# Column sums of the five transitions: from running sums on VectorE and GpSimd to one set of matmuls per tile

## The chip, the core and the metric

The kernel runs on one core of a Trainium2 chip. The core has a matrix engine (TensorE, "PE" in the rows; its weight loads are listed apart as "PEld"), VectorE ("DVE"), ScalarE ("ACT"), GpSimd ("POOL") and SyncE ("SP", which issues DMAs). The metric is the device time of one execution in microseconds (us); lower is better. All times here come from the hardware profiler on the chip or from timed runs.

## The reference, cut to what matters

A network of three layers on 256 tokens of 1024 features in fp32. Each of its residual steps ends with a sum over the 1024 features of each token: the layer norms need the sum and the sum of squares, the second block's norm after the mixer needs sums of squares.

```python
def layer_norm(x, g, b):
    xf = x.astype(jnp.float32)
    mu = jnp.mean(xf, axis=-1, keepdims=True)
    var = jnp.mean(jnp.square(xf - mu), axis=-1, keepdims=True)
    return ((xf - mu) * lax.rsqrt(var + EPS) * g + b).astype(x.dtype)
...
        x = layer_norm(ALPHA * x + (1.0 + g1[:, None, :]) * y, ln_g[l, 0], ln_b[l, 0])
        h = modulate(x, sh2, sc2)
        y = sq_relu_mlp(h, mlp_w1[l], mlp_w2[l])
        x = layer_norm(ALPHA * x + (1.0 + g2[:, None, :]) * y, ln_g[l, 1], ln_b[l, 1])
...
    mix = jnp.concatenate([o_dn, o_at.astype(o_dn.dtype)], axis=-1) @ w_out[l]
    h = h + rms_norm_2(mix, norm_mix_post[l])
    u = rms_norm_2(h, norm_mlp_pre[l])
```

## The kernel before, in words

Activations lie feature-major: 1024 features are eight tiles (m = 0 to 7) of 128 partitions by 256 tokens. Every big product keeps fp32 accuracy by three matmuls: `mm3` (L387 to L389) multiplies high part by high part, and each high part by the other's low part. ScalarE casts a weight's high part (`cast_hi`, L347) and VectorE, or in one place GpSimd, takes the low part (`cast_lo`, L352). In the rows `hi` and `lo` are a weight's parts, `oh`/`ol` and `acth`/`actl` the activation's, and `y` a product tile in PSUM, two tiles to a bank.

**Transitions.** Where one product ends and a norm must be known before the next begins, `tail` (L702) runs. There are five, called T1 to T5 here: T1 after `ev_out` (around 204 to 220 us), T2 after layer 0's MLP (396 to 414), T3 after `od_out` (527 to 551), T4 after layer 1's MLP (727 to 752), T5 after `b_out` (943 to 970). T1 to T4 are layer norms, closed by `ln_finish` or a sibling that uses it; T5 is `post_norm`. A transition holds back the last three weights (two in T3), multiplies all but the last of them into four tiles first, and then takes the tiles in the order 0, 2, 4, 6, 1, 3, 5, 7, each finished by the last weight: three matmuls for the first four tiles, nine for the later ones (six in T3); the scheduler may move the others ahead. When tile m is complete, VectorE forms the residual tile (`zn` in the rows, L633; `full` in T5, L1870) and ScalarE its square (`sq`, L635 and L1871; T5 also has `sqn`, L1872).

**Sums.** `totals` adds tiles up on an engine: the n-th tile of the group 0 to 3 onto the first (L556, L559), again for 4 to 6, and the eighth stays alone. Residuals are added on VectorE and squares on GpSimd; in T5 `full` on GpSimd, `sq` and `sqn` on VectorE. The running sums are the tiles `run`. Only at n = 7 does TensorE sum over features: `col_sum` (L543, recorded at L392) makes a 128x128 fp32 piece of the tile the stationary operand and multiplies it by a column of ones, two matmuls a tile (256 tokens), added up in the PSUM tile `tr`. Such a matmul has two records in the profile. `warm` (L392 with `zero`, PSUM tile `pj`) issues matmuls of zeros. Then VectorE reads `tr` (L585, T5 L1885) and the statistics follow.

**The other edits' places.** `tail` casts the first two weights of the next stage ahead: the low part of the second is GpSimd's. `rest1` (T3 and what follows) has two GpSimd operations on `metaT`, repeated eight times over: the cast L1704 and the subtraction L1705. They are written after T3, but stand in GpSimd's queue between T3's sums of squares. `mlp` calls `tick`, which draws pieces of side work (`self.fill`: the `ada` vector of the layer, then the residual) into the loop over j at a pace set by `n`.

Instructions are placed by a scheduler within each engine's queue, unless a stretch is marked as ordered by hand.

Of the kernel before, what the change touches and what calls it, by code (L numbers as in the profile page):

```python
# [10 lines left out]
F32 = mybir.dt.float32  # L11
F32R = mybir.dt.float32r
AF = mybir.ActivationFunctionType
OP = mybir.AluOpType
# [252 lines left out]
class Kern:  # L267
# [277 lines left out]
        for tb in range(2):  # L545
            self.mm(s[:, i + tb:i + tb + 1], x[:, 128 * tb:128 * tb + 128], self.ones[:, 0:1], False, last)

    def totals(self, s, i, eng):

        t, todo = [None], []  # L550

        def add(n, x):
            if n not in (0, 4, 7):
                if n in (1, 5):
                    y = self.T(self.lnp, (128, 256), f"run{i}{n}", bufs=1)
                    eng.tensor_tensor(y, t[0], x, op=OP.add)  # L556
                    t[0] = y
                else:
                    eng.tensor_tensor(t[0], t[0], x, op=OP.add)  # L559
            else:  # L560
                t[0] = x
            if n in (3, 6, 7):
                todo.append((t[0], n == 7))

        def rest():
            self.col_sum(s, i, *todo.pop(0))

        return add, rest

# [43 lines left out]
    def ln_finish(self, gate, mod):  # L613

        nc = self.nc
        c = SimpleNamespace()

        def begin():
            z = [self.T(self.resid, (128, 4, 256), "zn", bufs=2) for _ in range(2)]
            c.r = [z[m // 4][:, m % 4, :] for m in range(8)]  # L620
            c.gate = self.need(*gate)
            c.mod = mod()
            c.s = self.col_stats(1e-5)
            c.one, c.two = self.totals(c.s, 0, nc.vector), self.totals(c.s, 2, nc.gpsimd)

        def tile_(n, m, y):
            if y is None:
                if n == 7:
                    c.one[1]()
                    c.two[1]()  # L630
                return
            r = c.r
            nc.vector.scalar_tensor_tensor(r[m], y, c.gate[:, m:m + 1], self.xa[:, m, :], op0=OP.mult, op1=OP.add)  # L633
            sq = self.T(self.lnp, (128, 256), "sq", bufs=3)
            nc.scalar.activation(sq, r[m], AF.Square)  # L635
            c.one[0](n, r[m])
            c.two[0](n, sq)
            if n == 7:
                c.one[1]()
                c.two[1]()  # L640
                self.warm(2)
                c.one[1]()
                c.two[1]()

        def end(work):
            next(work, None)
            mu, rs = self.rstd_rows(c.s, 1024, True)
            next(work, None)
            c.mod(c.r, mu, rs, work)

        return begin, tile_, end

    def mod_apply(self, li, sc, sh):
# [48 lines left out]
    def tail(self, y, held, finish, following, before=lambda: None):  # L702


        nc = self.nc
        with self.ordered(MAN[4]):
            ws = [(*self.fetch(w, False), a) for w, a in held]
            nx = [self.arrive(n, True, False) for n in following[:4]]
            for n in following[4:]:
                self.pref[n] = self.load_raw(n, True)  # L710
            for w, e in zip(nx, (nc.vector, nc.gpsimd)):
                self.cast_hi(w)
                self.cast_lo(w, e)
            acts = before()
            self.idle = self.PS("pj")
            if acts is not None:
                ws[-1] = (*ws[-1][:2], acts)
            self.cast_hi(nx[2])
            for m in range(4):
                for wh, wl, a in ws[:-1]:  # L720
                    self.down(y, m, (wh, wl), *a)

            def work():
                self.cast_lo(nx[2], nc.vector)
                yield
                for part in range(2):
                    if len(nx) > 3:
                        self.cast_lo(nx[3], nc.vector, part)
                    yield

            for n, m in enumerate((0, 2, 4, 6, 1, 3, 5, 7)):
                if m > 3:
                    for wh, wl, a in ws[:-1]:
                        self.down(y, m, (wh, wl), *a)
                wh, wl, a = ws[-1]
                finish[1](n, m, None)
                self.down(y, m, (wh, wl), *a, last=True)
                finish[1](n, m, y[m])
                if n == 3:
                    for w in nx[3:]:  # L740
                        self.cast_hi(w)
            k = work()
            self.warm(1)
            finish[2](k)
            for _ in k:
                pass
        for n, w in zip(following, nx):
            self.done[n] = w[1], w[2]
# [81 lines left out]
                             k == 0 and j % 2 == 0, k == 7)  # L830
        return [(j, self.mlp_act(ps[j])) for j in range(4)]

    def mlp(self, l, finish, following, vectors):

        pend = self.mlp_head(l)
        y = self.y_tiles()
        self.fill = self.chain(*(self.ada(*lv) for lv in vectors), self.fill)
        n = 8 * len(vectors) + 8
        for j in range(4, 31):
            self.tick(n * (j - 3) // 26 - n * (j - 4) // 26)  # L840
            late = True if j > 28 else None
            pend.append((j, self.mlp_up(l, j, late)))
            while len(pend) > 1 and pend[0][0] < 29:
                i, a = pend.pop(0)
                self.down_all(y, self.fetch(f"dn{l}_{i}", late), a, i == 0)
        self.tick(n)
        finish[0]()
        self.done[f"up{l}_31"] = self.fetch(f"up{l}_31", True)
        self.tail(y, [(f"dn{l}_{i}", a) for i, a in pend] + [(f"dn{l}_31", None)], finish, following,
                  lambda: self.mlp_up(l, 31))  # L850
# [838 lines left out]
    def rest1(self, stop):  # L1689
        nc, tc, A = self.nc, self.tc, self.A  # L1690
        self.pieces = 6
        self.out_proj("od_out", range(4 + MORE1, 8), self.ln_finish((1, 2), self.mod_apply(2, (1, 4), (1, 3))),
                      self.mlp_first(1))
        self.dump("x3", self.xa)
        if stop == "x3":
            return
        with tc.tile_pool(name="phm1", bufs=1) as self.ph:
            self.pieces = 6

            self.mrep = [self.T(self.acts, (128, 8, 128), tag, F32R) for tag in ("oh", "ol")]  # L1700
            mh, ml = (t.rearrange("p k (e t) -> p k e t", e=8) for t in self.mrep)
            meta = self.metaT[:, :, None, :].to_broadcast([128, 8, 8, 16])
            with self.fenced():
                nc.gpsimd.tensor_copy(mh, meta)  # L1704
                nc.gpsimd.tensor_tensor(ml, meta, mh.bitcast(F32), op=OP.subtract)  # L1705
            self.mlp(1, self.last_ln((1, 5)), ['b_t0', 'b_t1', 'b_t2', 'b_c4', 'b_q0', 'b_c5', 'b_q1', 'b_c6'],
                     ((1, 5),))
        return True


    def meta_prep(self):
# [135 lines left out]
    def post_norm(self):  # L1847

        nc = self.nc
        post, ys = self.L["npmix"], [None] * 8  # L1850
        c = SimpleNamespace()

        def begin():
            c.s = self.PS("tr")
            self.mm(c.s[:, 0:6], self.ones, self.epsw, True, False)
            c.sums = [self.totals(c.s, 2 * i, nc.vector if i else nc.gpsimd) for i in range(3)]

        def rest():
            for x in c.sums:
                x[1]()  # L1860

        def tile_(n, m, y):
            if y is None:
                if n == 7:
                    rest()
                return
            ys[m] = y

            xs = [self.T(self.lnp, (128, 256), t, bufs=3) for t in ("full", "sq", "sqn")]
            nc.vector.scalar_tensor_tensor(xs[0], y, post[:, m:m + 1], self.xa[:, m, :], op0=OP.mult, op1=OP.mult)  # L1870
            nc.scalar.activation(xs[1], y, AF.Square)  # L1871
            nc.scalar.activation(xs[2], y, AF.Square, scale=post[:, m:m + 1])  # L1872
            for x, t in zip(c.sums, xs):
                x[0](n, t)
            if n == 7:
                rest()
                self.warm(2)
                rest()

        def end(work):  # L1880
            next(work, None)
# [17 lines left out]
            for m in range(9):  # L1899
# [7 lines left out]
                if m > 0:  # L1907
# [4 lines left out]
                    self.normed_halves(k, f, 0)  # L1912

        return begin, tile_, end

    def late_loads(self, pool, after):
# [839 lines left out]
```

## Time and profile before

| | |
|---|---|
| three runs | 1170.65, 1166.39, 1165.0 us; median 1166.39 us |
| the profiled execution's own time | 1162.97 us |
| its span in the trace | 1161.2 us (1.8 us lie around it) |
| TensorE's mean granted clock in it | 0.955 of full |

The profiled execution lies 3.4 us below the median of the runs. All rows below are from it. "Granted clock" is the speed that TensorE was allowed, as a share of full: the trace knows 1.00 (2.4 GHz) and 0.50 (1.2 GHz), and a stretch with both shows a value between.

### The profile page before, as it was taken

The page shows a single profiled execution, that of the slowest core. Times are in us where ns is not written, and L with a number is a line of the kernel's source. Part 1 is how long each engine was busy: PE and PEld are TensorE (multiplying, and loading weights), DVE is VectorE, ACT ScalarE, POOL GpSimd, SP SyncE. Part 2 cuts the span into 40 slices and gives each one's busy share as a digit, 9 for nine tenths or more (in the row PEclk, how much of TensorE's full clock was granted, in tenths as well). Part 3 has the DMA queues.
Part 4 walks back from the last instruction along what each step waited for, and adds up shares of the span by engine and source line. Part 5 has one row for each costly group of instructions (what it writes and reads, how often), then busy time and mean ns, then how long its engine had stood idle before and what let it go on. Part 6 is the DMA issues. An engine that isn't in the chain of part 4 may idle for free.

```text
span 1161.2 us, 20465 instructions
## 1 busy us (share of the span) xinstructions
PE 1073.1 (92%) x7766; PEld 975.4 (84%) x7766; DVE 840.5 (72%) x1672; ACT 595.3 (51%) x1240; POOL 269.3 (23%) x307
## 2 busy tenths in 40 slices
PE   2789889999999999997999999998899989999996
PEld 1667667999999978896999999887776888899995
DVE  7578985799886677877976555678986677655553
ACT  2456747464445445653754444557365354544442
POOL 3284673100000201324000000336644250000000
PEclk9799888999999989997999999899899997999998
DMA  9977643299996227636587553032120252765621
GB/s 344 316 266 271 210 155 112 89 404 349 331 336 229 97 90 294 211 135 235 202 287 237 183 179 119 1 109 92 55 66 27 92 200 68 252 189 182 189 83 37
DMA packets 60447, 212.58 MB, mean 183 GB/s; under 512 B 6619, under 2 KB 9084, under 8 KB 60348
## 3 DMA queue, kind: packets, MB, share of 16 engines
q1 hardware_dynamic: 59424, 209.43, 51.3%
q0 software_dynamic: 192, 0.79, 0.4%
q8 instruction: 61, 1.00, 0.3%
q10 hardware_dynamic: 732, 1.05, 0.3%
q14 instruction: 38, 0.31, 0.1%
HBM read 209.15 MB, written 1.84 MB: 182 GB/s over the span
## 4 chain that ended last, share of the span: by engine, by line
PE 68%; DVE 14%; DMA 5%; POOL 5%; issue 4%; ACT 3%; POOLq 0%; DVEq 0%; ACTq 0%; SPq 0%
PE y L387 10%; PE y L388 10%; PE y L389 10%; PE pj L387 7%; PE pj L389 7%; PE pj L388 7%; DMA raw<-in_ws 3%; PE tr L392 2%; DVE lo L352 2%; PE y L401 2%; DVE raw L478 1%; PE y L392 1%; PE pj L392 1%; DVE cva L2178 1%; POOL se L1457 1%
## 5 line engine op out<-in xcount | busy, mean ns | idle before, releaser
L366 DVE TENSOR_TENSOR lo<-raw,hi 128x1024 fp32r<-128x1024 f32 (+1 forms) x208 | 226.6, 1105 | 107.0 <-ACT hi L365 106.9
L365 ACT ACTIVATE hi<-raw 128x1024 fp32r<-128x1024 f32 (+1 forms) x208 | 195.3, 959 | 94.1 <-PE pj L388 76.4
L387 PE MATMUL pj<-hh,hi 128*128 128x256 f32 x768 | 216.7, 282 | 0.3
L388 PE MATMUL pj<-hl,hi 128*128 128x256 f32 x768 | 216.6, 282 | 0.2 <-DVE hl L611 0.2
L389 PE MATMUL pj<-hh,lo 128*128 128x256 f32 x768 | 215.7, 281 | 0.0
L352 DVE TENSOR_TENSOR lo<-raw,hi 128x1024 fp32r<-128x1024 f32 (+2 forms) x103 | 126.6, 1236 | 42.2 <-ACT hi L347 40.8
L387 PEld LDWEIGHTS pj<-hh,hi 128*128 128x128 f32 x768 | 145.1, 189 | 2.5 <-ACT relu L807 0.9
L388 PEld LDWEIGHTS pj<-hl,hi 128*128 128x128 f32 x768 | 144.9, 189 | 1.6 <-DVE hl L611 0.4
L389 PEld LDWEIGHTS pj<-hh,lo 128*128 128x128 f32 x768 | 145.2, 189 | 0.0
L388 PE MATMUL y<-actl,hi 128*128 128x256 f32 x512 | 144.3, 282 | 0.8 <-DVE actl L810 0.7
L387 PE MATMUL y<-acth,hi 128*128 128x256 f32 x512 | 144.0, 281 | 0.0
L389 PE MATMUL y<-acth,lo 128*128 128x256 f32 x512 | 143.7, 281 | 0.0
L352 POOL TENSOR_TENSOR lo<-raw,hi 128x512 fp32r<-128x512 f32 (+3 forms) x28 | 47.5, 1703 | 357.9 <-ACT hi L347 335.9
L347 ACT ACTIVATE hi<-raw 128x1024 fp32r<-128x1024 f32 (+2 forms) x107 | 110.8, 1043 | 27.1 <-DMA raw<-in_ws 16.1
L478 DVE CUSTOM_DVE_ANT_0 raw<-raw,cact 128x1024 f32<-128x1024 f32 x75 | 97.1, 1303 | 2.7 <-DMA raw<-in_ws 2.7
L388 PEld LDWEIGHTS y<-actl,hi 128*128 128x128 f32 x512 | 96.9, 189 | 1.5 <-DVE actl L810 1.4
L387 PEld LDWEIGHTS y<-acth,hi 128*128 128x128 f32 x512 | 97.1, 190 | 0.1
L389 PEld LDWEIGHTS y<-acth,lo 128*128 128x128 f32 x512 | 96.8, 189 | 0.0
L388 PE MATMUL y<-hl,hi 128*128 128x256 f32 x296 | 84.5, 286 | 0.0
L387 PE MATMUL y<-hh,hi 128*128 128x256 f32 x264 | 79.7, 302 | 3.9 <-ACT f L1588 2.2
L809 ACT ACTIVATE acth<-act 128x256 fp32r<-128x256 f32 x96 | 39.4, 416 | 83.5 <-DVE act L808 83.5
L389 PE MATMUL y<-hh,lo 128*128 128x256 f32 x264 | 76.8, 291 | 0.0
(658 smaller groups left out, 2486.3 us busy)
## 6 DMA issues: line engine op xcount, KB each, us to landing
raw<-in_ws SPq DMA_DIRECT2D x372, 512.0 KB, 4.7
bm<-bscr SPq DMA_DIRECT2D x4, 512.0 KB, 14.6
raw<-in_ws SPq DMA_DIRECT2D x4, 416.0 KB, 8.7
bm<-in_ws SPq DMA_DIRECT2D x3, 512.0 KB, 8.2
raw<-in_ws SPq DMA_DIRECT2D x3, 408.0 KB, 3.7
zn<-in_ws SPq DMA_DIRECT2D x2, 512.0 KB, 6.6
xa<-in_xT SPq DMA_DIRECT2D x2, 512.0 KB, 6.6
oh<-in_ws SPq DMA_DIRECT2D x2, 512.0 KB, 7.3
```

The source lines that it names most:

```text
L347: return self.nc.scalar.activation(w[1], w[0], AF.Copy)
L352: return eng.tensor_tensor(w[2][:, a:b], w[0][:, a:b], w[1][:, a:b].bitcast(F32), op=OP.subtract)
L365: i = nc.scalar.activation(hi[:, a:b], raw[:, a:b], AF.Copy)
L366: j = (lo_by or nc.vector).tensor_tensor(lo[:, a:b], raw[:, a:b], hi[:, a:b].bitcast(F32), op=OP.subtract)
L387: mm(out, lh, rh, start=start, stop=False, skip_group_check=True)
L388: mm(out, lh, rl, start=False, stop=False, skip_group_check=True)
L389: mm(out, ll, rh, start=False, stop=stop, skip_group_check=True)
L392: self.nc.tensor.matmul(out, l, r, start=start, stop=stop, skip_group_check=True)
L401: last = self.nc.tensor.matmul(out, l, r, start=start, stop=stop, skip_group_check=True)
L478: nc.vector.tensor_tensor_reduce(out=raw, in0=raw, in1=self.cact, op0=OP.mult, op1=OP.add, scale=0.5, scalar=0.0, accum_out=t)
L809: nc.scalar.activation(ah, f, AF.Copy)
L1457: nc.gpsimd.tensor_scalar(es[g][:, sl], es[g][:, sl], sm[:, tb, g:g + 1], 1.0, op0=OP.mult, op1=OP.mult)
```

## The change

`totals` no longer adds tiles. It keeps a list of finished tiles; before the last weight of tile n is multiplied, `rest(n - 2)` issues the column sums of all tiles up to the (n-2)-th on TensorE: the residual and its square, in T5 three tiles. After the last tile come those of the seventh, one `warm` matmul instead of two, and those of the eighth. The adds on VectorE and GpSimd (5 and 5 in each of T1 to T4, 10 and 5 in T5) are gone. The low part of the second weight cast ahead moves from GpSimd to VectorE. The two `metaT` operations become sixteen pieces of 128x128 that `mlp(1)` draws as side work, at 32 ticks in place of 16.

```diff
--- before.py
+++ after.py
@@ -545,25 +545,19 @@
-    def totals(self, s, i, eng):
-
-        t, todo = [None], []
-
-        def add(n, x):
-            if n not in (0, 4, 7):
-                if n in (1, 5):
-                    y = self.T(self.lnp, (128, 256), f"run{i}{n}", bufs=1)
-                    eng.tensor_tensor(y, t[0], x, op=OP.add)
-                    t[0] = y
-                else:
-                    eng.tensor_tensor(t[0], t[0], x, op=OP.add)
-            else:
-                t[0] = x
-            if n in (3, 6, 7):
-                todo.append((t[0], n == 7))
-
-        def rest():
-            self.col_sum(s, i, *todo.pop(0))
+    def totals(self, s, *cols):
+
+
+        todo = []
+
+        def add(n, *xs):
+            todo.append((n, xs))
+
+        def rest(until):
+            while todo and todo[0][0] <= until:
+                n, xs = todo.pop(0)
+                for i, x in zip(cols, xs):
+                    self.col_sum(s, i, x, n == 7)
 
         return add, rest
 
@@ -621,26 +615,21 @@
-            c.one, c.two = self.totals(c.s, 0, nc.vector), self.totals(c.s, 2, nc.gpsimd)
+            c.add, c.rest = self.totals(c.s, 0, 2)
 
         def tile_(n, m, y):
             if y is None:
-                if n == 7:
-                    c.one[1]()
-                    c.two[1]()
+                c.rest(n - 2)
                 return
             r = c.r
             nc.vector.scalar_tensor_tensor(r[m], y, c.gate[:, m:m + 1], self.xa[:, m, :], op0=OP.mult, op1=OP.add)
             sq = self.T(self.lnp, (128, 256), "sq", bufs=3)
             nc.scalar.activation(sq, r[m], AF.Square)
-            c.one[0](n, r[m])
-            c.two[0](n, sq)
+            c.add(n, r[m], sq)
             if n == 7:
-                c.one[1]()
-                c.two[1]()
-                self.warm(2)
-                c.one[1]()
-                c.two[1]()
+                c.rest(6)
+                self.warm(1)
+                c.rest(7)
 
@@ -708,9 +697,9 @@
-            for w, e in zip(nx, (nc.vector, nc.gpsimd)):
+            for w in nx[:2]:
                 self.cast_hi(w)
-                self.cast_lo(w, e)
+                self.cast_lo(w, nc.vector)
@@ -830,12 +819,12 @@
-    def mlp(self, l, finish, following, vectors):
+    def mlp(self, l, finish, following, vectors, more=()):
 
         pend = self.mlp_head(l)
         y = self.y_tiles()
-        self.fill = self.chain(*(self.ada(*lv) for lv in vectors), self.fill)
-        n = 8 * len(vectors) + 8
+        self.fill = self.chain(*(self.ada(*lv) for lv in vectors), self.fill, more)
+        n = 8 * len(vectors) + (24 if more else 8)
@@ -1696,16 +1685,22 @@
-
-            self.mrep = [self.T(self.acts, (128, 8, 128), tag, F32R) for tag in ("oh", "ol")]
-            mh, ml = (t.rearrange("p k (e t) -> p k e t", e=8) for t in self.mrep)
-            meta = self.metaT[:, :, None, :].to_broadcast([128, 8, 8, 16])
-            with self.fenced():
-                nc.gpsimd.tensor_copy(mh, meta)
-                nc.gpsimd.tensor_tensor(ml, meta, mh.bitcast(F32), op=OP.subtract)
             self.mlp(1, self.last_ln((1, 5)), ['b_t0', 'b_t1', 'b_t2', 'b_c4', 'b_q0', 'b_c5', 'b_q1', 'b_c6'],
-                     ((1, 5),))
+                     ((1, 5),), more=self.meta_eight())
         return True
+
+    def meta_eight(self):
+
+        nc = self.nc
+        self.mrep = [self.T(self.acts, (128, 8, 128), tag, F32R) for tag in ("oh", "ol")]
+        mh, ml = (t.rearrange("p k (e t) -> p k e t", e=8) for t in self.mrep)
+        meta = self.metaT[:, :, None, :].to_broadcast([128, 8, 8, 16])
+        for k in range(8):
+            with self.after(1):
+                nc.gpsimd.tensor_copy(mh[:, k], meta[:, k])
+            yield
+            nc.gpsimd.tensor_tensor(ml[:, k], meta[:, k], mh[:, k].bitcast(F32), op=OP.subtract)
+            yield
@@ -1853,16 +1848,11 @@
-            c.sums = [self.totals(c.s, 2 * i, nc.vector if i else nc.gpsimd) for i in range(3)]
-
-        def rest():
-            for x in c.sums:
-                x[1]()
+            c.add, c.rest = self.totals(c.s, 0, 2, 4)
 
         def tile_(n, m, y):
             if y is None:
-                if n == 7:
-                    rest()
+                c.rest(n - 2)
                 return
...
-            for x, t in zip(c.sums, xs):
-                x[0](n, t)
+            c.add(n, *xs)
             if n == 7:
-                rest()
-                self.warm(2)
-                rest()
+                c.rest(6)
+                self.warm(1)
+                c.rest(7)
```

TensorE in T1, in its order in the program. `zn` is a tile of the residual, `run` a running sum, `tr` the PSUM tile of the column sums, `y` a product. Before, from the last tile's last weight on:

```order
L392 MATMUL tr_2084<-ones_85,run_487_2178 128x1 x2
L392 MATMUL tr_2084<-ones_85,run_488_2180 128x1 x2
L387 MATMUL y_447_1978<-oh_1808,hi_466_2106 128x256
L388 MATMUL y_447_1978<-ol_1809,hi_466_2106 128x256
L389 MATMUL y_447_1978<-oh_1808,lo_467_2107 128x256
L392 MATMUL tr_4553<-eps_6_93,ones_85 128x4
L392 MATMUL tr_2084<-ones_85,run_493_2223 128x1 x2
L392 MATMUL tr_2084<-ones_85,run_494_2225 128x1 x2
```

After the change, in the middle of the same transition:

```order
L389 MATMUL y_447_1978<-oh_1808,lo_464_2099 128x256
L392 MATMUL tr_2084<-ones_85,zn_2077 128x1 x2
L392 MATMUL tr_2084<-ones_85,sq_2176 128x1 x2
L387 MATMUL y_447_1978<-oh_1808,hi_466_2106 128x256
L388 MATMUL y_447_1978<-ol_1809,hi_466_2106 128x256
L389 MATMUL y_447_1978<-oh_1808,lo_467_2107 128x256
L392 MATMUL tr_2084<-ones_85,zn_2078 128x1 x2
L392 MATMUL tr_2084<-ones_85,sq_2192 128x1 x2
```

Four column-sum matmuls (two rows of x2), a group, now stand ahead of nearly every tile's last products. Seen over the whole transition the order is: group, nine products, group, three, group, three, group, nine, group, nine, group, three, group, `warm`, group; in T3 six stand in place of nine. Before there were two groups of running sums and the group of the eighth tile. In T5 a group is six matmuls.

VectorE in T3, from the casts ahead on. `lo` is a weight's low part, `zn` a residual tile, `run` the running sum. Before:

```order
L352 TENSOR_TENSOR lo_1222_6199<-raw_1220_6196,hi_1221_6198 128x1024
L633 SCALAR_TENSOR_TENSOR zn_6169<-y_1174_5914,mod_750_3774,xa_120 128x256
L633 SCALAR_TENSOR_TENSOR zn_6169<-y_1175_5915,mod_750_3774,xa_120 128x256
L556 TENSOR_TENSOR run_1239_6250<-zn_6169 128x256
L633 SCALAR_TENSOR_TENSOR zn_6170<-y_1192_6016,mod_750_3774,xa_120 128x256
L352 TENSOR_TENSOR lo_1228_6207<-raw_1226_6204,hi_1227_6206 128x1024
L559 TENSOR_TENSOR run_1239_6250<-run_1239_6250,zn_6170 128x256
```

After:

```order
L352 TENSOR_TENSOR lo_1214_6209<-raw_1212_6206,hi_1213_6208 128x1024
L352 TENSOR_TENSOR lo_1217_6213<-raw_1215_6210,hi_1216_6212 128x1024
L625 SCALAR_TENSOR_TENSOR zn_6179<-y_1166_5924,mod_746_3779,xa_120 128x256
L625 SCALAR_TENSOR_TENSOR zn_6179<-y_1167_5925,mod_746_3779,xa_120 128x256
L352 TENSOR_TENSOR lo_1220_6217<-raw_1218_6214,hi_1219_6216 128x1024
L625 SCALAR_TENSOR_TENSOR zn_6180<-y_1184_6026,mod_746_3779,xa_120 128x256
```

The adds L556 and L559 are gone, and a second cast of a low part (from GpSimd) stands ahead of the first residual tile.

GpSimd in T3, before; `mss`, `se` and `dr` belong to other work, `oh`/`ol` from `metaT` are the two operations that move:

```order
L352 TENSOR_TENSOR lo_1225_6203<-raw_1223_6200,hi_1224_6202 128x1024
L556 TENSOR_TENSOR run_1240_6252<-sq_6242,sq_6248 128x256
L559 TENSOR_TENSOR run_1240_6252<-run_1240_6252,sq_6261 128x256
L559 TENSOR_TENSOR run_1240_6252<-run_1240_6252,sq_6272 128x256
L1704 CAST oh_6395<-metaT_4864 128x1024
L556 TENSOR_TENSOR run_1246_6291<-sq_6281,sq_6287 128x256
L1705 TENSOR_TENSOR ol_6396<-metaT_4864,oh_6395 128x1024
L559 TENSOR_TENSOR run_1246_6291<-run_1246_6291,sq_6300 128x256
L591 TENSOR_TENSOR st_6329<-va_6330,mhalf_83 128x2
```

After the change all but the last of these are gone from T3, where GpSimd has only the power (now L585) left, and the `metaT` pieces stand in the MLP that follows.

## Rows read from the trace of the kernel before

**Rows 1.** The page, part 1: busy time and share of each engine

```profile
PE 1073.1 (92%) x7766; PEld 975.4 (84%) x7766; DVE 840.5 (72%) x1672; ACT 595.3 (51%) x1240; POOL 269.3 (23%) x307
```

**Rows 2.** T1, T2, T4: length, busy (count) by engine, PEclk, DMA, GB/s

```profile
206.00:216.00 10.00, 10.00 (x90) 9.85 (x90) 6.91 (x15) 3.23 (x8) 3.67 (x5) 1.00 0.11 45
...
398.00:405.00 7.00, 7.00 (x61) 7.00 (x60) 6.09 (x14) 2.85 (x8) 3.05 (x4) 1.00 0.01 4
...
728.00:735.00 7.00, 7.00 (x62) 6.99 (x61) 5.93 (x13) 2.86 (x8) 3.73 (x6) 1.00 0.01 2
```

**Rows 3.** Chain that ended last, end of T1: start us, us, what

```profile
212.78 0.79 PE tr L392 x8
213.56 0.23 PE y L387
213.79 0.12 PE y L388
...
214.02 1.01 PE tr L392 x10
...
215.49 0.90 PE tr L392 x8
```

**Rows 4.** Timelines, end of T2: start us, us, instruction, [idle before<-releaser]

```profile
405.26 0.50 PE L392 MATMUL tr<-ones,run 128*128 128x1 f32 x4
...
408.31 0.16 DVE L585 TENSOR_SCALAR st<-tr 128x2 f32<-128x2 f32 x1 [2.37 <-PE tr L392]
```

**Rows 5.** Chain that ended last, end of T4

```profile
734.36 0.87 PE tr L392 x8
...
735.68 0.80 PE tr L392 x8
```

**Rows 6.** DVE and PE timelines, T3

```profile
527.51 1.23 DVE L352 TENSOR_TENSOR lo<-raw,hi 128x1024 fp32r<-128x1024 f32 x1 [0.86 <-ACT hi L347]
...
529.83 1.72 DVE L556 TENSOR_TENSOR run<-zn 128x256 f32<-128x256 f32 x1
...
532.00 0.38 PE L387 MATMUL y<-oh,hi 128*128 128x256 f32 x1 [0.74 <-DVE zn L633]
...
534.66 0.39 PE L387 MATMUL y<-oh,hi 128*128 128x256 f32 x1 [1.57 <-DVE zn L633]
...
538.65 1.01 PE L392 MATMUL tr<-ones,run 128*128 128x1 f32 x4 [1.44 <-DVE run L559]
...
543.10 1.01 PE L392 MATMUL tr<-ones,run 128*128 128x1 f32 x4 [3.44 <-POOL run L559]
...
546.52 0.16 DVE L585 TENSOR_SCALAR st<-tr 128x2 f32<-128x2 f32 x1 [4.06 <-PE tr L392]
```

**Rows 7.** POOL timeline, T3: the longer of the two operations that move

```profile
539.14 2.77 POOL L1705 TENSOR_TENSOR ol<-metaT,oh 128x1024 fp32r<-128x1024 f32 x1
```

**Rows 8.** Chain that ended last, end of T5

```profile
957.71 0.21 PE y L388
...
958.14 2.35 PE tr L392 x12
...
961.37 2.37 PE tr L392 x12
```

**Rows 9.** PE timeline, T5

```profile
951.00 0.39 PE L387 MATMUL y<-oh,hi 128*128 128x256 f32 x1 [2.00 <-ACT sqn L1872]
```

**Rows 10.** Stretches at half clock and one just ahead, columns as before

```profile
536.90:550.50 13.60, 8.72 (x33) 6.38 (x32) 7.78 (x13) 1.01 (x3) 6.47 (x5) 0.50 0.33 125
...
741.70:745.00 3.30, 2.92 (x26) 2.84 (x26) 1.88 (x6) 3.17 (x7) 2.42 (x5) 1.00 0.00 0
...
745.10:751.90 6.80, 5.70 (x22) 4.36 (x22) 3.43 (x11) 2.89 (x8) 0.70 (x1) 0.50 0.01 4
...
956.80:970.30 13.50, 12.91 (x52) 10.46 (x52) 7.19 (x21) 2.40 (x7) 1.91 (x3) 0.50 0.14 48
```

**Rows 11.** A stretch of layer 0's MLP

```profile
234.00:246.00 12.00, 11.26 (x96) 11.05 (x96) 12.00 (x26) 6.45 (x16) 1.67 (x2) 1.00 1.03 419
```

## The prediction

> **What bounds the kernel now.** Read the page's first part first: TensorE is busy 92% of the span, no other engine over 72% [rows 1]. A share over the span says nothing about five short stretches, so the next view is the table of windows laid over the transitions. In T1, T2 and T4 TensorE and its weight loads are busy without a gap, with the clock at 1.00, while VectorE is at 6.9 of 10 us and GpSimd at under 4 [rows 2]. The running sums that the change removes are therefore hidden there, and whatever goes onto TensorE is paid. The chain of waits at T1's end has TensorE in every piece [rows 3]. T3 is another case: TensorE waits four times, 0.74 and 1.57 us for VectorE's residual tiles, 1.44 for VectorE's running sum, 3.44 for GpSimd's [rows 6]. T5 lies between: TensorE waits 2.00 us for the first square [rows 9] and then runs out its end at half clock [rows 8, 10].
>
> **Price of a group.** Eight records of one-column sums (four matmuls, a group of T1 to T4) take 0.79 us in T1, 0.10 a record; the product behind them takes 0.23 in place of 0.12, so 0.11 is lost in the change over: 0.90 in all [rows 3]. In T5 a group has 12 records; at half clock these took 2.35 us, twice the 12 x 0.099 = 1.18 of full clock [rows 8]. Products go 0.12 and 0.21 [rows 3, 8]. That weight loads of 128 columns, not the moving column, set the 0.10 is my reading, since PEld is as full as PE in rows 2.
>
> The Trainium skill ("TensorE: Matmul & The Clock Gate", section "LDWEIGHTS (loading the stationary operand)") puts a load at columns / 1.2 ns, here about 107 ns a record, whatever the moving width. At full clock the trace agrees (99 ns); at half clock it doesn't (2.35 / 12 = 196 ns), and the skill names no clock in that formula. By that page of the skill T5's groups would not slow, and T5 would cost about +5 us where the sum below has +12.5; the measurement decides.
>
> **T1, T2, T4.** Before, one group stands between products and one or more at the end; now six between and two at the end: five more in T1 and T4 at 0.90, +4.5 each, and the same in T2. The end gets shorter. Before, T1's last product is followed by 1.01, 0.46 up to 215.49 (two zero matmuls) and 0.90, 2.37 us in all [rows 3], T4's by 2.12 (734.36 to 736.48) [rows 5], T2's by 3.02 (405.26 to just before the read at 408.31) [rows 4]. After: group, one zero matmul, group, 0.79 + 0.22 (half of the 0.46) + 0.79 = 1.80. So T1 +4.5 - 0.57 = +3.9, T4 +4.2, T2 +3.3: **+11.4** with the clock at full.
>
> The thinning itself can take the clock. One-column sums alone ran 3.3 us at 1.00, with 26 matmuls, and the stretch behind them was granted 0.50 [rows 10]; so such work does not hold the clock for long, but does not lose it at once. In T1, T2 and T4 it would be lost in the thin middle (group, three products, group, three, group), with about 6 us of work behind it that would double: 0 to +6 for each. The nine-product stretches behind the middle are dense, so I take 1 each, **+3**.
>
> **T3.** The 0.74, 1.57, 1.44 and 3.44 us of waiting [rows 6] are what the change can take away: GpSimd's sums of squares, behind the 2.77 us subtraction [rows 7], no longer end the transition, nor does VectorE's first add of 1.72 us. One wait grows. The second cast now stands ahead of the first residual tile: 527.51 + 1.23, then as long again and up to 0.4 of waiting for ScalarE's high part, so the first tile comes at some 530.4, its square behind ScalarE's work at 531, and the first group is done about 531.7. Behind it TensorE has 7 groups (5.5), 24 products (2.8), six changes (0.7) and a zero matmul (0.2): 9.2, the end at 540.9, against 546.5 [rows 6]: -5.5 at full clock. But TensorE was at 0.50 from 536.9 on there [rows 10], and the new stream is thin too. If the clock falls at a time f, the end is at 2 x 541 - f: 548 for f = 534 (+1.5), 545 for 537 (-1.5). I take f near 536: **0**, bounds -5.5 and +2. So the gain of the waits is given back.
>
> **T5.** The first group needs the square that TensorE waits for until 951.00 [rows 9], and stands ahead of those products, so it is done about 951.4 (its first columns can go earlier). Then 7 groups of 1.18 (8.3), 36 products (4.2), six changes (0.7), a zero matmul: 13.4, the end at 964.8. Before it was 963.74 [rows 8]: +1.1 at full clock. Before, half clock ruled 956.8 to 970.3 [rows 10], after two waits and the sums; now TensorE has stood still for 2 us by 951 and then brings 12 records of sums for every three to nine products. If it falls at f, the end is 2 x 964.8 - f: 976.6 for 953, 973 for 956.6. I take 953.4, **+12.5**, bounds +1.1 and +13.5. Stretches of 12 records and nine products (2.35 + 1.9 us at half clock) are too thin, I judge by rows 10, to bring the clock back before the statistics.
>
> **Layer 1's MLP.** At 32 ticks the dots of `ada` are drawn twice as fast early on. In layer 0's MLP, where they run, VectorE is full for 12 of 12 us and TensorE at 11.26 [rows 11]; 0.74 in 12 us is the most that such a stretch lost. Bounds 0 to 0.75, taken **+0.5**. The `metaT` pieces lie on GpSimd, busy 1.67 of those 12 us, beside TensorE; without that cover they would cost about the old subtraction's 2.77 us [rows 7] and its cast. The second cast on VectorE costs nothing in T1, T2 and T4 (3 of 10 us free, and five adds gone); were the first tile late there too, up to its 1.23 us would be paid each time.
>
> **Sum.** 11.4 + 3 + 0 + 12.5 + 0.5 = 27.4 on the profiled execution's 1162.97 us: 1190.4. The median of the runs is 3.4 higher, so by it the same sum gives 1193.8; I say **1190**, as the profiled execution is one of the quicker. From the terms' bounds (half of what the clock can do either way) its own range is 1181 to 1199.
>
> **Rivals.** *The clock holds everywhere.* Then 11.4 - 5.5 + 1.1 + 0.5 = +7.5, 1170.5 (1174 on the median). For: sums alone kept 1.00 for 3.3 us [rows 10]. Against: T3 and T5 fell already with fewer sums. *It falls in T1, T2 and T4 early and stays:* 3 x 6 in place of 3, 1205. For: their middle is as thin as T5's. Against: before it come 24 products without a gap, and the nine-product stretches follow.
>
> *Faster: sums hide among the products.* If a one-column matmul between products costs less than in a run of its own, because its load goes ahead beside the running product, a group costs p in place of 0.90. With the clock at full the balance is +7.5 - 30 x (0.90 - p): 15 groups of T1, T2 and T4, six of T3, six larger ones of T5 counted as nine. It turns at p = 0.65; at 0.40 it gives -7.5, 1155. For: only runs of eight or more are in the trace. Against: PEld is full in rows 2, so there is no free load time, and products too need one each.
>
> The same page of the Trainium skill, section "Back-to-back issue gap", gives a sustained 81 ns a matmul for 128 moving columns, load included; eight records would be 0.65, an estimate from that page. No row here shows less than 99 ns.
>
> *The change doesn't do what it says* is excluded by the order: the adds are gone and the groups stand between products.
>
> **Chances.** Forecast (half clock through T5, briefly elsewhere) 0.63; clock at full 0.16; half clock everywhere 0.12; hidden sums 0.06; 0.03 left for others. The range 1172 to 1203 leaves out the hidden sums, half of the full-clock case and a part of the slowest. Faster or slower counts from 0.5%, 5.8 us, about what a measurement tells: below 1160.6 only the hidden sums, 0.07; up to 1172.2 more than half of the full-clock case, 0.10; slower 0.83.
>
> **What would show it.** In the changed profile: groups of 0.8 us between products in T1, T2 and T4, with PE still without gaps and the read of `tr` 3 to 4 us later after the first group; T3 without waits for `run`, its end within 2 us of before; T5's groups at 2.35 us and its end 10 us or more later, with 0.50 from about 953. Wrong would be a group under 0.65 us between products, or a clock of 1.00 in the whole of T5, or TensorE idle for residual tiles in T1.

## The result, and the profile after

The changed kernel takes 1200.53 us in the median (four runs, 1198.06 to 1204.7) against 1168.18 (four runs): a ratio of 1.0275, interval 1.0243 to 1.0306, so slower by some 32 us. 1190 was forecast, with 1172 to 1203 as the range. The profiled execution of the changed kernel took 1198.22 us, with a span of 1196.4 and a mean granted clock of 0.945.

The read of the finished column sums (L585 before, L579 after, in T5 L1885 and L1874) is a mark that both traces share. It divides the span:

| stretch | before, us | after, us | difference | forecast |
|---|---|---|---|---|
| start to T1's read | 216.42 | 222.76 | +6.3 | +3.9 |
| T1's read to T2's | 191.89 | 195.15 | +3.3 | +3.3 |
| T2's to T3's | 138.21 | 140.68 | +2.5 | 0 |
| T3's to T4's (with layer 1's MLP) | 189.98 | 196.32 | +6.3 | +4.7 |
| T4's to T5's | 227.25 | 244.29 | +17.0 | +12.5 |
| T5's to the end | 197.4 | 197.2 | -0.2 | 0 |

Of the first row 2.1 us arose before T1 (its first matmul into `tr` at 206.62, before the change at 204.55), so T1 itself is +4.3. The rows add up to 35.2 us. The forecast's 3 us for a clock that falls in T1, T2 or T4 stand in none of them.

The page of the changed kernel, part 1, which answers to [rows 1]: 40 us more on TensorE, less on VectorE and GpSimd.

```profile
PE 1112.9 (93%) x7981; PEld 1018.1 (85%) x7981; DVE 825.9 (69%) x1647; ACT 596.0 (50%) x1240; POOL 239.7 (20%) x291
```

Windows of the changed kernel over T1, T2 and T4, from the first group to the read, and over T3 and T5, from within the second group to the read (length, busy time by engine, granted clock, DMA share, GB/s):

```profile
211.00:222.50 11.50, 11.50 (x104) 11.47 (x104) 2.90 (x6) 2.95 (x8) 0.00 (x0) 1.00 0.01 1
406.30:417.70 11.40, 11.40 (x103) 11.37 (x102) 2.91 (x6) 2.91 (x8) 0.00 (x0) 1.00 0.00 0
743.30:754.70 11.40, 11.40 (x103) 11.37 (x102) 2.90 (x6) 2.91 (x8) 1.00 (x3) 1.00 0.01 1
542.20:558.40 16.20, 16.20 (x79) 16.11 (x78) 3.80 (x8) 2.50 (x6) 3.22 (x11) 0.50 0.51 201
976.60:999.00 22.40, 22.40 (x106) 22.31 (x107) 2.42 (x5) 3.75 (x10) 0.00 (x0) 0.50 0.20 80
```

VectorE is down to a quarter of T1, T2 and T4, against 69 to 87% of the stretches in [rows 2], GpSimd is empty or nearly so, and TensorE with its weight loads is full, now with thinner work. T3 and T5 ran at 0.50 from their second group to the read.

TensorE's timeline in the middle of T1: two groups, each of a residual and its square, between which three products stand.

```profile
212.90 0.50 PE L392 MATMUL tr<-ones,zn 128*128 128x1 f32 x4
213.26 0.58 PE L392 MATMUL tr<-ones,sq 128*128 128x1 f32 x4
214.15 0.50 PE L392 MATMUL tr<-ones,zn 128*128 128x1 f32 x4
214.51 0.58 PE L392 MATMUL tr<-ones,sq 128*128 128x1 f32 x4
```

From group to group it is 214.15 - 212.90 = 1.25 us; three products at 0.117 us leave 0.90 for a group with the change over, the price taken from [rows 3].

The chain that ended last, T5's end, answers to [rows 8]: a group at 2.35 us behind every three or nine products.

```profile
990.81 2.35 PE tr L392 x12
993.16 0.42 PE y L387
993.58 0.21 PE y L388
993.80 0.21 PE y L389
994.01 2.35 PE tr L392 x12
996.36 0.45 PE pj L392
996.81 2.37 PE tr L392 x12
```

T3 of the changed kernel on VectorE, ScalarE, TensorE and GpSimd (timelines; it answers to [rows 6, 7]):

```profile
537.59 1.06 ACT L347 ACTIVATE hi<-raw 128x1024 fp32r<-128x1024 f32 x1 [1.49 <-DMA raw<-in_ws]
538.68 1.23 DVE L352 TENSOR_TENSOR lo<-raw,hi 128x1024 fp32r<-128x1024 f32 x1 [1.32 <-ACT hi L347]
539.82 0.87 DVE L625 SCALAR_TENSOR_TENSOR zn<-y,mod,xa 128x256 f32<-128x256 f32 x2
540.36 0.61 PE L392 MATMUL tr<-ones,zn 128*128 128x1 f32 x4 [2.73 <-DVE zn L625]
...
555.18 0.54 POOL L1700 CAST oh<-metaT 128x128 fp32r<-128x128 f32 x2 [27.02 <-PE y L389]
559.55 0.86 POOL L1702 TENSOR_TENSOR ol<-metaT,oh 128x128 fp32r<-128x128 f32 x2
560.37 0.69 POOL L585 TENSOR_TENSOR st<-va,mhalf 128x2 f32<-128x2 f32 x1
561.12 1.22 PE L392 MATMUL y<-p_first,st 128*128 128x128 f32 x4 [1.09 <-POOL st L585]
```

Two things are to be seen. ScalarE casts the second weight's high part (L347) and VectorE takes its low part (L352). That weight arrives late (ScalarE waits 1.49 us for its DMA), its cast on VectorE waits for ScalarE, and the first residual tile stands behind that cast: TensorE stops for 2.73 us. And the `metaT` pieces do not run in the MLP, where the text on the change puts them. All sixteen follow T3's last product, ahead of the power of T3's own statistics (L585 on GpSimd), for which TensorE then waits 1.09 us.

### The profile page after: what moved, and what is told of

Same layout as the page of the kernel before. It is cut to its first block, busy times and chain, and to the rows that moved or that the text cites. A ratio compares the mean times of both kernels' runs of the same rounds, so it can differ in the third digit from the quotient of the medians.

```text
span 1196.4 us, 20830 instructions
## 1 busy us (share of the span) xinstructions
PE 1112.9 (93%) x7981; PEld 1018.1 (85%) x7981; DVE 825.9 (69%) x1647; ACT 596.0 (50%) x1240; POOL 239.7 (20%) x291
## 4 chain that ended last, share of the span: by engine, by line
PE 48%; issue 18%; DVE 9%; POOL 3%; ACT 2%; DMA 1%; POOLq 0%; SPq 0%; DVEq 0%; ACTq 0%
PE y L387 7%; PE y L389 6%; PE y L388 6%; PE pj L387 5%; PE pj L388 5%; PE pj L389 5%; PE tr L392 3%; PE y L401 1%; DVE lo L352 1%; DVE cva L2167 1%; PE y L392 1%; DMA raw<-in_ws 1%; PE d L392 1%; PE sc L392 1%; POOL se L1627 1%
## 5 line engine op out<-in xcount | busy, mean ns | idle before, releaser
L352 DVE TENSOR_TENSOR lo<-raw,hi 128x1024 fp32r<-128x1024 f32 (+2 forms) x108 | 128.6, 1198 | 42.6 <-ACT hi L347 40.7
L347 ACT ACTIVATE hi<-raw 128x1024 fp32r<-128x1024 f32 (+2 forms) x107 | 110.7, 1042 | 28.4 <-DMA raw<-in_ws 18.2
L796 ACT ACTIVATE relu<-pj 128x256 f32<-128x256 f32 x96 | 35.0, 371 | 57.7 <-PE pj L389 57.7
```

The costliest lines, as they stand in the source:

```text
L347: return self.nc.scalar.activation(w[1], w[0], AF.Copy)
L352: return eng.tensor_tensor(w[2][:, a:b], w[0][:, a:b], w[1][:, a:b].bitcast(F32), op=OP.subtract)
L796: nc.scalar.activation(r, p, AF.Relu)
```

## The experiments

The lengths below are from each run's profiled execution; the ratios are to the kernel before, the time in brackets the interval. "T2's read to T3's" and the like mean the marks of the table.

**One edit undone: the second cast back on GpSimd.**

```diff
-            for w in nx[:2]:
+            for w, e in zip(nx, (nc.vector, nc.gpsimd)):
                 self.cast_hi(w)
-                self.cast_lo(w, nc.vector)
+                self.cast_lo(w, e)
```

> The changed kernel with one edit undone: the low part of the second weight cast ahead is GpSimd's again. Theory A (the moved cast holds back the first residual tile in T3 and T5, since it waits on VectorE's queue for a weight that arrives late): TensorE's wait ahead of T3's first group falls from 2.73 us to under 1, the one of T5 from 2.33 to under 1, and the time falls by 3 to 5 us. Theory B (only the added column sums on TensorE and its clock cost time): under 1 us of change.

1198.56 us, ratio 1.0268 (1.0229 to 1.0308): 2 us below the changed kernel, within what the runs scatter. T2's read to T3's is 138.9 in place of 140.7. TensorE's timeline in T3:

```profile
537.26 0.61 PE L392 MATMUL tr<-ones,zn 128*128 128x1 f32 x4 [0.26 <-DVE zn L625]
537.73 0.36 PE L392 MATMUL tr<-eps,ones 128*128 128x4 f32 x2
538.96 0.61 PE L392 MATMUL tr<-ones,sq 128*128 128x1 f32 x4 [0.86 <-ACT sq L627]
```

In T3 theory A holds: 1.1 us of waiting in place of 2.73. In T5 it fails: the first group still waits 3.00 us for `full`, so the late tile there is not the moved cast's doing. The cast is worth 1.8 us by T3's marks, not 3 to 5, and the 2 us of the whole can't be told from nothing.

**T5 alone as before.** `post_norm` keeps the old `totals` (here `running`), all else is as after the change.

```diff
+    def running(self, s, i, eng):
...
-            c.add, c.rest = self.totals(c.s, 0, 2, 4)
+            c.sums = [self.running(c.s, 2 * i, nc.vector if i else nc.gpsimd) for i in range(3)]
...
```

> The changed kernel with T5 alone as before: running sums on VectorE and GpSimd, column sums only at the end. Theory A (T5 costs what its groups take at half clock): 12 to 15 us less, about 1187. Rival (T5's loss is the late first tile, 2.3 us of waiting): 2 to 4 us less.

1185.18 us, 15.4 below the changed kernel, ratio 1.0142 (1.0097 to 1.0188). That is just over theory A's upper edge; a late first tile would not do it.

**T5 alone with column sums a tile**, T1 to T4 with running sums: the complement.

```diff
+    def running(self, s, i, eng):
...
-            c.add, c.rest = self.totals(c.s, 0, 2)
+            c.one, c.two = self.running(c.s, 0, nc.vector), self.running(c.s, 2, nc.gpsimd)
...
```

> The changed kernel with running sums again in T1 to T4, and column sums a tile in T5 alone. Theory A (T1, T2 and T4 cost 0.90 us for each of five more groups, 11.4 us with what their ends save; T3 about 5): 14 to 18 us less than the changed kernel, about 1184, and T1, T2 and T4 as long as before. Rival (the terms are not separate: most of the loss is one clock effect that T5 starts): within 5 us of the changed kernel.

1176.87 us, 23.7 below the changed kernel, ratio 1.0075 (1.0048 to 1.0101). More came off than expected, by 6 us, yet T1's read to T2's is 191.1 and T2's to T3's 135.1, so the four transitions carry their own loss. T4's read to T5's is 250.7, so T5 alone is not quicker than in the changed kernel (244.3); but this execution, at 1184.16 us, was the slowest of the ten. By the ratios the new sums in T5 alone leave a loss of 8.8 us and those in T1 to T4 alone 16.6, together 25 where the whole change loses 32. Each of the three ratios is uncertain by 3 to 5 us, so the runs can't tell whether the two parts add up.

**Zeros to hold the clock.** In T3 and T5 matmuls of zeros ahead of the first group (8) and behind each of the first six groups (`hold` is 1 in T3, 2 in T5): 34 in all, where the expectation counts 28.

```diff
             while todo and todo[0][0] <= until:
                 n, xs = todo.pop(0)
+                if hold and n == 0:
+                    self.warm(8)
                 for i, x in zip(cols, xs):
                     self.col_sum(s, i, x, n == 7)
+                if n < 6:
+                    self.warm(hold)
...
-            c.add, c.rest = self.totals(c.s, 0, 2, 4)
+            c.add, c.rest = self.totals(c.s, 0, 2, 4, hold=2)
```

> The changed kernel with matmuls of zeros added: in T5 8 ahead of the first group and 2 behind each of the next ones up to the sixth, in T3 8 and 1. The added work is 28 matmuls of 0.22 us, 6.2 us at full clock, of which those ahead of the first group fall into waits. Theory A (half clock doubles groups and products): granted clock 1.00 through T3 and T5, a group of T5 at 1.2 us, T3 shorter by some 5 us and T5 by some 8 after the added work, together 1186 to 1190. Rival (a group takes 2.35 us because loads are slow there, whatever the clock): no gain, 1201 to 1206.

1197.03 us, ratio 1.026 (1.0223 to 1.0298). Windows of that run over T1, T2 and T3, first group to read:

```profile
206.10:222.90 16.80, 16.80 (x106) 16.70 (x104) 3.00 (x7) 3.04 (x8) 0.00 (x0) 0.68 0.01 2
407.30:423.50 16.20, 16.20 (x104) 16.11 (x102) 2.93 (x7) 2.98 (x8) 0.00 (x0) 0.69 0.00 0
545.70:557.20 11.50, 11.50 (x101) 11.30 (x101) 5.46 (x10) 4.13 (x9) 1.66 (x6) 1.00 0.88 358
```

T3 is at 1.00 and takes 11.6 us from its first group to the read, with the zeros in it, where the changed kernel takes 18.2 without them: theory A for T3, shown. In T5 the clock fell all the same (0.70 from the first group to the read), so that half of the forecast was missed, and the whole gained 3.5 us, not 10 to 15. And T1 and T2, whose code is untouched, fell to 0.68 in this execution and took 16.9 and 16.3 us in place of 11.8 and 11.6. That is the second rival of the prediction, in some executions.

**More zeros in T5:** 12 ahead of the first group and 4 behind each of the first six; its edit is shown against the run before.

```diff
-                    self.warm(8)
+                    self.warm(8 if hold == 1 else 12)
...
-            c.add, c.rest = self.totals(c.s, 0, 2, 4, hold=2)
+            c.add, c.rest = self.totals(c.s, 0, 2, 4, hold=4)
```

> The changed kernel with more zeros: in T5 12 ahead of the first group and 4 behind each of the next up to the sixth (0.9 us a group at full clock), in T3 8 and 1 as before. Theory A (T5's column sums run at half clock only because too little is streamed among them): granted clock 1.00 through T5, from its first group to the read of the sums in 17 to 19 us in place of 26, the whole 9 to 13 us faster than the changed kernel, about 1189. Rival (zeros cost what they win in T5): 1195 to 1203.

1193.66 us, ratio 1.023 (1.0188 to 1.0271). Windows of T4 and T5, and then a piece of the chain in T5:

```profile
744.90:761.10 16.20, 16.20 (x103) 16.11 (x102) 2.90 (x6) 2.90 (x8) 1.45 (x3) 0.69 0.00 0
980.20:999.90 19.70, 19.70 (x159) 17.37 (x158) 4.32 (x9) 5.73 (x16) 0.00 (x0) 1.00 0.42 169
```

```profile
983.53 1.23 PE tr L392 x12
984.76 0.89 PE pj L392 x4
```

Now T5 is at 1.00 to its end, a group takes 1.23 in place of 2.35, and the transition 19.85 us (980.18 to the read) in place of 26.25 (972.95 to 999.20), with some 5 us of zeros in it. So the clock made T5's groups slow, and not loads that are slow at any clock. The whole gained 7, not 9 to 13, and its interval still overlaps the changed kernel's: in the profiled execution T4 fell to 0.69 (+4.7) and T3 to 0.54 in spite of its zeros. The zeros do two things at once, they fill the wait ahead of the first group and they stand among the groups; no run separates the two.

**32 columns in place of one.** The same sums, streamed 32 times over.

```diff
+WIDE = 32
...
+    def wide_sum(self, s, i, x, last):
+
+        for tb in range(2):
+            self.mm(s[:, WIDE * (i + tb):WIDE * (i + tb + 1)], x[:, 128 * tb:128 * tb + 128], self.ones[:, 0:WIDE], False, last)
...
-                    self.col_sum(s, i, x, n == 7)
+                    self.wide_sum(s, i, x, n == 7)
...
```

> The changed kernel with 32 columns of ones streamed per column sum in place of one (the same sums, 32 times over; the readers take one of the copies). Theory A (the weight load of 128 columns sets 0.10 us a record, not the moving side): a group of T1 stays at 0.8 us and the time within 3 us. Rival (the price is that of the moving side or of a fixed start): a group of eight records grows by 8 x 32 / 2.4 ns = 0.1 us or more, a loss of 5 us or more over 40 groups. The clock may hold better, since more columns move: then T3 and T5 get shorter.

1198.96 us, ratio 1.0273 (1.0226 to 1.0321). TensorE's timeline in T1:

```profile
209.79 0.53 PE L394 MATMUL tr<-ones,zn 128*128 128x32 f32 x4
210.16 0.61 PE L394 MATMUL tr<-ones,sq 128*128 128x32 f32 x4
211.04 0.53 PE L394 MATMUL tr<-ones,zn 128*128 128x32 f32 x4
```

From group to group 211.04 - 209.79 = 1.25, the same as with one column. The moving side is free at this size. That the load of the stationary tile sets the price fits with PEld being full, but a fixed price for each matmul would look the same here, so this is not shown. T3 and T5 were at 0.54 and 0.51 from the first group to the read, so 32 columns did not hold the clock either.

**The side edits alone:** running sums as before, the cast on VectorE, the `metaT` pieces and the 32 ticks as after.

```diff
-            for w, e in zip(nx, (nc.vector, nc.gpsimd)):
+            for w in nx[:2]:
...
-                     ((1, 5),))
+                     ((1, 5),), more=self.meta_eight())
```

> The kernel before with the side edits alone: both first low parts cast on VectorE, the two operations on the meta tokens in pieces in layer 1's MLP at 32 ticks; the sums stay on VectorE and GpSimd. Theory A (the loss is the column sums on TensorE): within 4 us of the kernel before either way; in T3 TensorE's wait of 3.44 us for GpSimd's sum goes, while the second cast delays the first residual tile by about 2 us. Theory B (the moved cast and the ticks carry a good part of the loss): 5 us or more slower than before.

1164.05 us, ratio 0.9982 (0.9956 to 1.0008): no difference that can be told. The loss is the column sums'. T2's read to T3's is 135.8 (before 138.2), T3's to T4's 192.0 (before 190.0): what T3 gains is lost behind its read. The wait for GpSimd's sum did not go, as expected, but fell from 3.44 to 2.52 us: the `metaT` pieces run in T3 here too, among GpSimd's sums of squares.

**The ticks alone.**

```diff
-        n = 8 * len(vectors) + 8
+        n = 8 * len(vectors) + (24 if l == 1 else 8)
```

> The kernel before with one thing changed: 32 ticks in place of 16 in layer 1's MLP, so the side work there is drawn twice as fast (the meta operations stay whole in T3). Theory A (the pace of the side work, not the meta pieces, lengthens this MLP): from T3's read of the sums to T4's about 192 us in place of 190.0, and 1 to 3 us slower. Theory B (the pieces on GpSimd cost the time): 190 us there, no change.

1165.74 us, ratio 0.9999 (0.9972 to 1.0025); T3's read to T4's is 190.2. The pace costs nothing that can be told. Theory A fell, and theory B's 190 us came out. What the pieces cost is read from the traces, where they stand ahead of T3's power in GpSimd's queue and not in the MLP.

**Can a part of it pay?** First the kernel before, with the `metaT` pieces of the change and zeros in the waits of T3 and T5:

```diff
+                if gate == (1, 2):
+                    self.warm({4: 4, 5: 7, 6: 2, 7: 5}.get(n, 0))
...
+                if n == 4:
+                    self.warm(9)
...
```

> The kernel before (running sums, second cast on GpSimd) with the meta operations moved as in the change and with matmuls of zeros put into the waits of T3 (24) and T5 (17), 0.22 us each at full clock. Theory A (T3's last wait is GpSimd behind the meta subtraction, and half clock doubles what follows): granted clock 1.00 through T3 and T5, T3 shorter by 3 to 6 us, T5 by 2 to 4, together 5 to 10 us faster than before. Rival (the waits are set by VectorE and ScalarE whatever the clock, and zeros come on top): 0 to 5 us slower.

1166.27 us, ratio 0.998 (0.9951 to 1.001). From the first sums to the read the clock rose from 0.57 to 0.73 in T3 and from 0.56 to 0.73 in T5; from T4's read to T5's it was 229.5, against 227.3 before. No gain: the 5 to 10 us were a miss.

Then column sums a tile in T3 alone, where TensorE waits for the adders. The cast stays on GpSimd, the pieces are drawn one a step beside the old ticks; with zeros (8, then 1 behind each of the first six groups), without, and with zeros in T5's waits too:

```diff
+                if gate == (1, 2):
+                    c.rest(n - 2)
+                    return
...
+                if HOLD and n == 0:
+                    self.warm(8)
```

> The kernel before, but with column sums a tile on TensorE in T3 alone, 8 matmuls of zeros ahead of the first group and one behind each of the next six; the meta operations in pieces in layer 1's MLP, one a step, at the old 16 ticks; second cast on GpSimd. Theory A (sums a tile are right where TensorE waits for the adding engines, if the clock is held): clock 1.00 in T3, from T2's read to T3's some 134 us in place of 138, the whole 4 to 8 us faster than before. Rival (TensorE's share grows, the wait goes elsewhere): within 3 us of before.

> As the run before it, without the zeros. Theory A (in T3 the clock decides whether sums a tile pay): clock near 0.6 in T3, T2's read to T3's 138 to 139 us, within 3 us of before and 3 to 6 us behind the run with zeros. Rival (the waits taken away decide): as fast as the run with zeros.

> As the run with column sums and zeros in T3, with zeros also in the waits of T5 (9 ahead of the fifth tile's last products, 4 behind the seventh tile), where the running sums stay. Theory A: the clock is held longer in T5, from T4's read to T5's 225 us in place of 227, 2 us faster than without. Rival (the zeros are late or in the way): no faster.

| T3's sums a tile | us | ratio (interval) | clock in T3 | T2's to T3's | T3's to T4's |
|---|---|---|---|---|---|
| with zeros | 1168.15 | 1.0012 (0.9991 to 1.0034) | 1.00 | 133.1 | 193.5 |
| without | 1171.73 | 1.0041 (1.0018 to 1.0063) | 0.61 | 141.1 | 191.5 |
| zeros in T5 too | 1168.4 | 1.002 (0.9999 to 1.0041) | 1.00 | 133.9 | 193.3 |

The clock decides in T3, as expected: 11.5 us from first group to read at 1.00, 18.8 at 0.61, and 3.6 us between the medians. But the 5 us that the first variant wins up to T3's read do not reach the end, and the 4 to 8 us that were expected of it did not come. Its GpSimd and TensorE behind T3's last product:

```profile
540.71 0.54 POOL L1745 CAST oh<-metaT 128x128 fp32r<-128x128 f32 x2 [9.64 <-PE y L391]
545.09 0.86 POOL L1747 TENSOR_TENSOR ol<-metaT,oh 128x128 fp32r<-128x128 f32 x2
545.90 0.70 POOL L612 TENSOR_TENSOR st<-va,mhalf 128x2 f32<-128x2 f32 x1
546.65 1.23 PE L394 MATMUL y<-p_first,st 128*128 128x128 f32 x4 [3.25 <-POOL st L612]
```

The pieces begin when T3's last product frees their tiles and hold the power back; the faster T3 ends, the longer TensorE waits for it, here 3.25 us of the 3.5 by which T3's read to T4's is longer than before. The zeros in T5's waits brought nothing (232.3 from T4's read to T5's, 225 was expected). No version here beats the kernel before; one with the pieces moved behind T3's power was not tried.

## Why the prediction held, and where its steps were off

**The sum.** 27.4 us was forecast on the profiled execution, and 35.2 measured there; the terms below say where. Of these, 2.1 arose ahead of T1 and 3.5 ahead of T5's first group. The medians differ by 32.4. The forecast of 1190 missed 1200.53 by 10.5: 5 of it in the terms, and 5 because the sum was set on an execution of 1162.97 us where the median of the runs is now 1168.18.

**T1, T2, T4.** Right, by mechanism and size: 0.90 a group between products, TensorE without a gap, +4.3, +3.3, and of T3's to T4's +6.3 some 4.3 (196.3 against the 192.0 of the side edits alone). The rival in which sums hide among the products (0.06) is excluded by the 1.25 us between groups. By the 81 ns of the Trainium skill ("TensorE: Matmul & The Clock Gate", section "Back-to-back issue gap") eight records would take 0.65 us, an estimate from that page; these groups show 0.81 (212.90 to 213.71, where the next product starts), and the measurement decides.

**The thinning, +3.** The price was right as a mean, and wrong for any one execution: in six profiled kernels with column sums in T1, T2 and T4, 15 of 18 transitions stayed at 1.00 and three fell to 0.68 or 0.69, each for 4.7 to 5.0 us more. That is 0.8 a transition, where 1 was taken. In the profiled execution of the changed kernel none of the three fell.

**T3, 0 with bounds of -5.5 and +2.** The four waits went, as forecast, but the term came out at +2.5, past its upper bound. The step that failed is the start of the first group. The first tile was put at about 1.6 us behind the first cast's end, with up to 0.4 of waiting for the high part; in the trace the second cast waited 1.32 us for a high part that itself waited for the weight's DMA, and the first group started 2.73 us after TensorE ran dry. The clock then fell at 542.2, 1.8 us behind the start of that group, and not midway. At full clock the -5.5 was right in kind: with zeros, T2's read to T3's was 133.7 and 133.1 against 138.2.

**T5, +12.5.** The mechanism was right, and T5's own size nearly: half clock from the second group on, 2.35 us a group as in [rows 8], and from the end of TensorE's first wait to the read 26.25 us against 12.75 before (951.00 to 963.75), +13.5. The other 3.5 of the +17.0 lie ahead of that, from T4's read to the end of the wait: 218.0 us against 214.5. Five runs with running sums in T5 took 216.0 to 219.7 there, so these 3.5 are not shown to be the change's; that the row came out so far above its term is in part the execution that stands for before. One step was off: the sum had the first group done 0.4 us behind the wait, and in the trace the whole group starts behind it.

```profile
972.95 0.60 PE L392 MATMUL tr<-ones,full 128*128 128x1 f32 x4 [2.33 <-DVE full L1860]
```

In the medians T5 is worth 15.4 us when undone and 8.8 when changed alone, each uncertain by 3 to 5 us. A record of T5's groups took 196 ns at half clock and 103 at full (1.23 us for 12). By the load time of the Trainium skill ("TensorE: Matmul & The Clock Gate", section "LDWEIGHTS (loading the stationary operand)"), 107 ns for 128 columns by a formula that names no clock, T5 would have cost about +5, an estimate; the measurement decides against it.

**Layer 1's MLP, +0.5, and the `metaT` pieces at nothing.** The ticks cost nothing that can be told (190.2 us from T3's read to T4's against 190.0), while with all side edits the stretch was 2.0 longer. The pieces were counted as GpSimd work beside the MLP; in GpSimd's queue they stand ahead of T3's power, not in the MLP as the text on the change says, and TensorE waits for it 1.09 us in the changed kernel and 3.25 us in the three runs where T3 stayed at 1.00. No such wait stands in the trace of before.

**The other rivals.** The clock did not hold everywhere: T3 and T5 were at 0.50, which the runs with zeros show to be worth 6.6 us in T3 (18.2 against 11.6) and 6.4 in T5 (26.25 against 19.85), the zeros already paid. Nor did it fall everywhere: T1, T2 and T4, where TensorE did not wait ahead of the first group, kept 1.00. Behind a wait of 2.73 and 2.33 us it fell in T3 and T5; whether the wait or the thin groups did it is open. The three transitions that fell in other runs had no wait ahead, and with the cast undone T3 still fell to 0.62, with waits of only 0.26 and 0.86 us.

## What to carry to other kernels

A column sum on the matrix engine took two records of 0.10 us for each 128x128 piece, with 1 or with 32 columns streamed. Between dense products on an engine that has no gap this was paid in full, 0.90 us a group, while the adds that it replaced had cost TensorE next to nothing in T1, T2 and T4, though VectorE was 69 to 87% busy there. Thin work also puts the granted clock at risk, and then groups and products take nearly twice as long (1.23 and 2.35 us, 0.12 and 0.21): price such a stretch at both clocks. When an operation is moved to another queue, or to another place in its own, look up what it will wait for there and which instruction then stands behind it; twice here the cost of a move lay in that, 1.8 us for the cast and 1.09 to 3.25 for the `metaT` pieces.

## What the runs showed of the hardware that was not expected

Streaming 32 columns in place of one costs nothing: 1.25 us from group to group either way. And the same code of T1 can take 11.8 us at a clock of 1.00 or 16.9 at 0.68, in executions of kernels that do not differ up to there.
